# Down projection as seven block products, with its weight sums made in DRAM

## The chip, the cores and the metric

The kernel runs on one core of a Trainium2 chip. TensorE (PE) multiplies matrices, VectorE (DVE), ScalarE (ACT) and GpSimd (POOL) do elementwise work, and SyncE (SP) issues most transfers; POOL's queue issues others. 16 DMA engines carry all of them. PEld is TensorE's loading of stationary operands, which overlaps its matmuls. The time is the device time of one execution in microseconds (us), as the median of several runs. The profile is one further execution.

## The reference

One layer of an encoder block on 512 tokens of 1024 features in float32, with 16 learned meta tokens in front. Cut to what matters:

```
xn = rmsnorm(h); proj = xn @ w_in          # q, k, v of two kinds of attention, 8 heads each
y_sb = stick_breaking(...) @ w_br_sb       # sb heads
y_df = differential(...) @ w_br_df         # df heads
h = h + (gate0 * y_sb + gate1 * y_df) @ w_out
hn = rmsnorm(h)
h = h + (silu(hn @ w_ffn_gate) * (hn @ w_ffn_up)) @ w_ffn_down     # 1024 -> 2816 -> 1024
y = rmsnorm(h)                              # meta tokens dropped
```

The change is in the last product, the down projection: 512 tokens x 2816 by 2816 x 1024.

## The kernel before

The kernel works through the layer in stages: the eight sb heads, the eight df heads (the projections of the next head are cut into units that are popped between the steps of this one), the gates, the output projection, the FFN's gate and up products, the down projection, and the last norm.

Every float32 operand is split into a high and a low part of float32r, so that one product takes three matmuls (L227 high by high, L228 low activations by high weights, L229 high activations by low weights). For a weight tile ScalarE casts the high part (wh, L75) and VectorE subtracts it to get the low one (wl, L76). The same two lines split activations (da).

Weights come through one list, `stream`, in order of use. `stage_one` (L128 to L145) issues the next load on SP's queue into one of three buffers (wst). How far ahead loads and splits run is set by two constants, READY for split tiles and STAGE for loads. In the down projection `rows(("down", half, k0), ...)` makes 22 tiles of 128 x 2 x 512.

The down projection is the function `accumulate` (L1007), called once per half of the 1024 columns. Tokens are stationary, 128 at a time, and 512 columns of weights stream past: 22 k-tiles x 4 token tiles x 3 matmuls per half. The last token tile of the second half is cut into two pieces of 256 columns, so that the end of the kernel is short. VectorE adds the banks onto hres (L1036), ScalarE squares for the norm, POOL multiplies by the gain (L1260, L1261), ScalarE scales, SP writes the output.

The inputs of the down projection are the transposed activations aT, 22 k-tiles of 128 x 512 tokens, made by the FFN.

Also touched by what follows is `turn()` (L462 to L478), run once per head: TensorE transposes v, POOL copies 4 x 16 tail columns of vT into v_s (L475), TensorE transposes v_s (L476), and ScalarE copies the result:

```
for t in range(NQ):
    nc.gpsimd.tensor_copy(v_s[:, 32 * t:32 * t + NM], vT[:, (t + 1) * P:(t + 1) * P + NM])
nc.tensor.transpose(p5[:, 0:P], v_s, ident)
nc.scalar.copy(vf[:, 1], p5[:, 0:P])
```

Each engine works through its own instructions in order. Up to L921 the order of PE, DVE and ACT is written out by hand; after that a scheduler orders each engine, and it orders POOL and SP throughout. POOL's queue carries the y parts (L731 writes, L733 adds onto them in DRAM) and the loads of hres (L1004). A transfer on POOL's queue signals one of eight completion semaphores in turn (DMASW0 to DMASW7 in the order shown below).

Of the kernel before, what the change touches and what calls it, by code (L numbers as in the profile page):

```python
# [40 lines left out]
def block_kernel(ctx: ExitStack, tc: tile.TileContext, x, meta, norm_mix_g, w_in, w_gate, b_gate,  # L41
# [15 lines left out]
    def mm_tile():  # L57
        return ps_mm.tile([P, 512], F32, tag="mm", name="mm")
# [4 lines left out]
    def z_tile():  # L63
        return ps_z.tile([P, 2, 512], F32, tag="z", name="z")
# [18 lines left out]
    def rows(key, view, c0, k0):  # L83
        stream.append((key, view, c0, 512, k0, k0 + 2))
# [27 lines left out]
    for f in range(NFF):  # L112
        cols(("fg", f), w_fg, f * P)
        cols(("fu", f), w_fu, f * P)
    for half in range(2):
        for k0 in range(0, NFF, 2):
            rows(("down", half, k0), w_fd, half * 512, k0)

    at_of = {c[0]: n for n, c in enumerate(stream)}
    first_ffn = at_of["fg", 1]  # L120
    staged, loaded = [], {}
    fpools = {}
    ops = {}
# [4 lines left out]
    def stage_one():  # L128
        n = len(staged)
        if n == len(stream):  # L130
            return False
        key, view, c0, cw, k0, k1 = stream[n]

        if key[0] == "fu" and key[1]:
            if "w" not in fpools:
                return False
            st = fpools["w"].tile([P, KT, P], F32, tag="wsu", bufs=2, name="wsu")
        elif sevens(key) and key[2] == 1:
            st = fpools["a"].tile([P, KT, P], F32, tag="wsu", name="wsu")
        else:  # L140
            st = wpool.tile([P, k1 - k0, cw], F32, tag="wst", bufs=3, name="wst")
        staged.append(st)
        for a, b in ((0, 4), (4, 8)) if n < 2 else ((0, k1 - k0),):
            nc.sync.dma_start(st[:, a:b], view[:, k0 + a:k0 + b, c0:c0 + cw])
        return True  # L145

    def stage(upto):
        while len(staged) < upto and stage_one():
            pass

    def parts(n):
        k, _, _, cw, k0, k1 = stream[n]
        loaded[k] = tuple(wpool.tile([P, k1 - k0, cw], F32R, tag=t, name=t) for t in ("wh", "wl"))
        return loaded[k]

    def generic(n):
# [67 lines left out]
    def mm3(ps, pairs, start=True, stop=True, skip=False):  # L224
        n = len(pairs)
        for i, (ah, al, bh, bl) in enumerate(pairs):
            nc.tensor.matmul(ps, lhsT=ah, rhs=bh, start=(start and i == 0), stop=False, skip_group_check=skip)  # L227
            nc.tensor.matmul(ps, lhsT=ah, rhs=bl, start=False, stop=False, skip_group_check=skip)  # L228
            nc.tensor.matmul(ps, lhsT=al, rhs=bh, start=False, stop=(stop and i == n - 1), skip_group_check=skip)  # L229
# [695 lines left out]
    for br in range(2):  # L925
        name, head = (("y_sb", sb_head), ("y_df", df_head))[br]
        if br:
            nc.gpsimd.memset(a_s, 0.0)
            y_out.append(xtp.tile([P, KT, SEQ], F32, tag="y_sb", name="y_out"))
        for h in range(NH):  # L930
            if (br, h) == (0, 0):
                tB["t"] = opool.tile([P, 2, 2, 4, HL], F32R, tag="y_df", name="tB", bufs=1)
                sums = sum_units()
            if (br, h) == (0, 4):
                df_constants()
            if h % 2 == 0:
# [67 lines left out]
        nc.gpsimd.dma_start(hres[:, t], xv[:, t])  # L1004
    ssq = [small.tile([P, 2], F32, tag=f"ssq{t}", bufs=2, name="ssq") for t in range(NQ)]

    def accumulate(pool, name, act, nk, half, tail, done, banks, pieces=None):  # L1007
# [6 lines left out]
        extra = z_tile()[:, 0] if pieces else None  # L1014

        def step(k, t, c0, c1):
# [3 lines left out]
            mm3((acc[t] if c0 == 0 else extra)[:, c0:c1],  # L1020
                [(ah[:, q], al[:, q], wh[:, k % 2, c0:c1], wl[:, k % 2, c0:c1])], k == 0, k == nk - 1)


        def cuts(t):
            return ((0, 256), (256, 512)) if t == NQ - 1 and pieces else ((0, 512),)

        for k in range(nk - tail):
            for t in range(NQ):
                for c0, c1 in cuts(t):
                    step(k, t, c0, c1)  # L1030
        for t in range(NQ):
            for c0, c1 in cuts(t):
                for k in range(nk - tail, nk):
                    step(k, t, c0, c1)
                cs = slice(half * 512 + c0, half * 512 + c1)
                nc.vector.tensor_tensor(hres[:, t, cs], hres[:, t, cs], (acc[t] if c0 == 0 else extra)[:, c0:c1], op=ALU.add)  # L1036
                sq = pool.tile([P, 512], F32, tag="y_sb", bufs=2, name="sq")
                s0, s1 = ssq[t][:, 0:1], ssq[t][:, 1:2]
                nc.scalar.activation(sq[:, c0:c1], hres[:, t, cs], AF.Square, accum_out=(s1 if half else s0))
                if half == 0:  # L1040
                    nc.vector.tensor_scalar(s0, s0, 1.0 / D, EPS, op0=ALU.mult, op1=ALU.add)
                elif c1 < 512:
                    nc.vector.scalar_tensor_tensor(s0, s1, 1.0 / D, s0, op0=ALU.mult, op1=ALU.add)
                if pieces:
                    pieces(t, cs)
# [90 lines left out]
    with tc.tile_pool(name="ffn", bufs=1) as fp:  # L1136
# [10 lines left out]
        jobs += [(generic, n) for n in range(at_of["down", 0, 0], len(stream))]  # L1147
        made = {"n": 0}

        def ready(upto):  # L1150
# [56 lines left out]
        first(2)  # L1207
        first_out(2)
        dw, acts = None, []

        def act_parts(upto):

            for i in range(len(acts), min(2 * NFF, upto)):
                pool, tag, bufs = ((dw, "da", 4), (fw, ("wsu", "s21")[i % 2], 2))[i % 8 < 4]
                a = pool.tile([P, 2, SEQ], F32R, tag=tag, bufs=bufs, name="da")
                split(a[:, 0], a[:, 1], aT[:, i % NFF])
                acts.append(a)

        def act(half, k):
            act_parts(half * NFF + k + 3)  # L1220
            return acts[half * NFF + k][:, 0], acts[half * NFF + k][:, 1]

        for f in range(1, NFF):
            ready(at_job(c2, f) + 3)
# [19 lines left out]
        fpools["down"] = down_weights  # L1244
        ov = out[0].rearrange("(t p) d -> p t d", p=P)

        def finish(t):
# [7 lines left out]
        outs = []  # L1255

        def gained(t, cs):
            if len(outs) == t:
                outs.append(dw.tile([P, D], F32, tag="outs", name="outs", bufs=2))
                nc.gpsimd.tensor_tensor(outs[t][:, 0:512], hres[:, t, 0:512], gF[:, 0:512], op=ALU.mult)  # L1260
            nc.gpsimd.tensor_tensor(outs[t][:, cs], hres[:, t, cs], gF[:, cs], op=ALU.mult)  # L1261

        ssq = [small.tile([P, 2], F32, tag=f"ssq{t}", bufs=2, name="ssq") for t in range(NQ)]
        accumulate(dw, "down", act, NFF, 0, 0, lambda t: None, "z")
        accumulate(dw, "down", act, NFF, 1, 6, finish, "mm", gained)
        inner.close()


# [27 lines left out]
```

## Time and profile before

| what | value |
|---|---|
| median of 3 runs | 987.93 us (987.78 to 987.96) |
| span of the profiled execution | 987.0 us |
| PE busy | 963.9 us (98%) |
| DVE busy | 675.5 us (68%) |
| ACT busy | 572.6 us (58%) |
| POOL busy | 166.4 us (17%) |
| DMA, 16 engines, SP's queue q1 | 30.0% |
| DMA, POOL's queue q0 | 12.5% |
| first to last matmul of the down projection | 855.3 to 979.0 us |

"Busy" is the time in which an engine executed. The chain that ended last is followed back from the last instruction, each step to what released it. A row of a group gives line, engine, operation, output and input, their shapes, count, then busy time and mean of one, then idle time of the engine before these instructions and what ended it. A row of the timeline gives start, length, engine, line, operation, and in brackets the idle time before and its releaser.

### The profile page before, as it was taken

Reading aid. Unit: us, or ns where it says so; the run is one execution under the profiler, and the core shown is the slowest. Engines: PE = TensorE matmul, PEld = TensorE weight load, DVE = VectorE, ACT = ScalarE, POOL = GpSimd, SP = SyncE. Lnnn points to the kernel's source line nnn. Section 1 sums busy time; section 2 is a strip of 40 time slices with the busy share of each in tenths; the row PEclk is TensorE's granted clock in tenths of the full one; section 3 lists DMA queues with packets and bytes.
Section 4 is the critical chain, followed back from the end, with each engine's and each line's share of the span. In section 5 each row is a group of like instructions: output and inputs, shape, how many; then the busy total and the mean of one; then the engine's idle time right before and its main releaser. Section 6 shows DMA issues by size and latency. Waiting matters only on the chain.

```text
span 987.0 us, 16198 instructions
## 1 busy us (share of the span) xinstructions
PE 963.9 (98%) x6213; PEld 869.3 (88%) x6213; DVE 675.5 (68%) x1244; ACT 572.6 (58%) x1091; POOL 166.4 (17%) x216
## 2 busy tenths in 40 slices
PE   7999999999999999999999999989999999999996
PEld 4998888898899998899878888879999999988885
DVE  8898687766566876667724433798888888754644
ACT  5666666666566666666763433675555555743533
POOL 4010111111243322442224320000000000000103
PEclk9999999999999999999999999999999999999999
DMA  7312434455565533656659623232434333333212
GB/s 217 86 43 65 128 102 112 95 125 130 129 130 129 130 113 124 129 117 140 130 136 287 195 90 103 64 107 87 128 87 119 97 110 105 110 104 107 86 43 86
DMA packets 140240, 114.12 MB, mean 116 GB/s; under 512 B 4961, under 2 KB 115714, under 8 KB 140162
## 3 DMA queue, kind: packets, MB, share of 16 engines
q1 hardware_dynamic: 129810, 89.29, 30.0%
q0 software_dynamic: 10192, 23.73, 12.5%
q8 instruction: 49, 0.80, 0.3%
q14 instruction: 29, 0.24, 0.1%
q10 hardware_dynamic: 160, 0.07, 0.0%
HBM read 89.87 MB, written 18.87 MB: 110 GB/s over the span
## 4 chain that ended last, share of the span: by engine, by line
PE 88%; DVE 6%; ACT 4%; DMA 1%; issue 1%; POOL 0%; SPq 0%; DVEq 0%; ACTq 0%; POOLq 0%
PE mm L229 20%; PE mm L227 20%; PE mm L228 20%; PE z L227 6%; PE z L229 6%; PE z L228 6%; PE z L638 1%; PE z L637 1%; PE tr L493 1%; PE tr L469 1%; PE z L493 1%; ACT wh L75 1%; DVE s L576 1%; PE z L521 1%; DVE wl L76 0%
## 5 line engine op out<-in xcount | busy, mean ns | idle before, releaser
L76 DVE TENSOR_TENSOR wl<-wst,wh 128x1024 fp32r<-128x1024 f32 (+1 forms) x150 | 169.3, 1133 | 110.6 <-ACT wh L75 110.5
L75 ACT CAST wh<-wst 128x1024 fp32r<-128x1024 f32 (+1 forms) x150 | 146.0, 973 | 124.6 <-PE mm L228 68.4
L227 PE MATMUL mm<-xT_h,wh 128*128 128x264 f32 (+2 forms) x656 | 214.3, 327 | 0.2 <-ACT xT_h L831 0.2
L228 PE MATMUL mm<-xT_l,wh 128*128 128x264 f32 (+2 forms) x656 | 213.6, 326 | 0.4 <-DVE xT_l L832 0.3
L229 PE MATMUL mm<-xT_h,wl 128*128 128x264 f32 (+2 forms) x656 | 212.8, 324 | 0.0
L227 PEld LDWEIGHTS mm<-xT_h,wh 128*128 128x128 f32 x656 | 123.9, 189 | 10.0 <-ACT xT_h L831 1.0
L228 PEld LDWEIGHTS mm<-xT_l,wh 128*128 128x128 f32 x656 | 123.7, 189 | 10.0 <-DVE xT_l L832 0.6
L229 PEld LDWEIGHTS mm<-xT_h,wl 128*128 128x128 f32 x656 | 123.7, 189 | 9.9
L228 PE MATMUL mm<-hT_l,wh 128*128 128x256 f32 x284 | 80.5, 284 | 0.7 <-DVE hT_l L1079 0.7
L227 PE MATMUL mm<-hT_h,wh 128*128 128x256 f32 x284 | 80.1, 284 | 0.6 <-DVE sg L1174 0.6
L229 PE MATMUL mm<-hT_h,wl 128*128 128x256 f32 x284 | 80.1, 283 | 0.0
L641 DVE CUSTOM_DVE_ANT_0 pr<-z,bias 128x144 f32<-128x144 f32 (+3 forms) x64 | 30.9, 502 | 34.9 <-PE z L638 34.8
L228 PEld LDWEIGHTS mm<-hT_l,wh 128*128 128x128 f32 x284 | 53.7, 189 | 1.2 <-DVE hT_l L1079 1.1
L227 PEld LDWEIGHTS mm<-hT_h,wh 128*128 128x128 f32 x284 | 53.4, 189 | 0.9 <-DVE sg L1174 0.8
L475 POOL COPY v_s<-vT 128x16 f32<-128x16 f32 x64 | 26.3, 440 | 162.5 <-DVE vT L405 78.2
L229 PEld LDWEIGHTS mm<-hT_h,wl 128*128 128x128 f32 x284 | 53.6, 189 | 0.0
L227 PE MATMUL mm<-o_h,wh 128*128 128x512 f32 x128 | 53.1, 415 | 0.0
L229 PE MATMUL mm<-o_h,wl 128*128 128x512 f32 x128 | 50.8, 397 | 0.0
L228 PE MATMUL mm<-o_l,wh 128*128 128x512 f32 x128 | 50.1, 392 | 0.3 <-DVE o_l L709 0.3
L1260 POOL TENSOR_TENSOR outs<-hres,gF 128x512 f32<-128x512 f32 x4 | 5.1, 1291 | 262.2 <-DVE hres L1036 261.3
L227 PE MATMUL mm<-t_h,wh 128*128 128x256 f32 x168 | 47.5, 282 | 1.3 <-ACT wh L75 1.0
L228 PE MATMUL mm<-t_l,wh 128*128 128x256 f32 x168 | 47.2, 281 | 1.1 <-DVE t_l L1094 1.1
(328 smaller groups left out, 2538.5 us busy)
## 6 DMA issues: line engine op xcount, KB each, us to landing
wst<-in_w_in_dram SPq DMA_DIRECT2D x40, 512.0 KB, 4.7
wst<-in_w_ffn_gate_dram SPq DMA_DIRECT2D x22, 512.0 KB, 3.8
wst<-in_w_ffn_down_dram SPq DMA_DIRECT2D x22, 512.0 KB, 3.5
wsu<-in_w_ffn_up_dram SPq DMA_DIRECT2D x21, 512.0 KB, 3.8
y_df<-y_out POOLq DMA_DIRECT2D x32, 256.0 KB, 5.1
wst<-in_w_gate_dram SPq DMA_DIRECT2D x16, 512.0 KB, 5.4
wst<-in_w_br_sb_dram SPq DMA_DIRECT2D x8, 512.0 KB, 4.7
wst<-in_w_br_df_dram SPq DMA_DIRECT2D x8, 512.0 KB, 3.8
```

What stands on the lines that cost most here:

```text
L75: (hi_copy or nc.scalar.copy)(hi, src)
L76: (lo_eng or nc.vector).tensor_tensor(lo, src, hi.bitcast(F32), op=ALU.subtract)
L227: nc.tensor.matmul(ps, lhsT=ah, rhs=bh, start=(start and i == 0), stop=False, skip_group_check=skip)
L228: nc.tensor.matmul(ps, lhsT=ah, rhs=bl, start=False, stop=False, skip_group_check=skip)
L229: nc.tensor.matmul(ps, lhsT=al, rhs=bh, start=False, stop=(stop and i == n - 1), skip_group_check=skip)
L469: nc.tensor.transpose(pt[:, j * P:(j + 1) * P], vT[:, j * P:(j + 1) * P], ident)
L475: nc.gpsimd.tensor_copy(v_s[:, 32 * t:32 * t + NM], vT[:, (t + 1) * P:(t + 1) * P + NM])
L493: nc.tensor.transpose(pt[:, (t - j) * P:(t - j + 1) * P], blocks(t, j * P, (j + 1) * P), ident)
L521: nc.tensor.matmul(ps.rearrange("p (t q) -> p t q", q=P)[:, :, lo_rows:P], lhsT=vf[:, 1], rhs=a_s[:, 0:4 * qn], start=False, stop=True)
L576: nc.vector.tensor_tensor_scan(f, f, f, 0.0, op0=ALU.add, op1=ALU.bypass)
L637: nc.tensor.matmul(o, lhsT=q[c][:, qs], rhs=k[c][:, 0, k0:k1], start=True, stop=False)
L641: nc.vector.tensor_tensor_reduce(po, zz, bb, scale=1.0, scalar=-3.0e38, op0=ALU.add, op1=ALU.max, accum_out=mx[:, t, c:c + 1])
```

## The change

The down projection becomes a 2 x 2 x 2 block product made of seven products instead of eight. Blocks are 11 k-tiles x 512 columns of weights (a) and 256 tokens x 11 k-tiles of activations (b):

```
DOWN = (("a11", "b11", 0), ("a12", "b21", 1), ("s1", "t1", 2), ("s2", "t2", 0), ("s4", "b22", 2), ("s3", "t3", 0),
        ("a22", "t4", 0))
```

Each entry is weights, activations, and the accumulator that takes the product. Four weight blocks are sums: s1 = a21 + a22, s3 = a21 + a11, s2 = a11 + s1, s4 = a12 + s2. They are made in DRAM by transfers on POOL's queue: 24 copies out of w_ffn_down into the DRAM tiles (d...) and 24 that accumulate (8 block jobs of 6 tiles each; five tiles are of 512 KB, the sixth of 256 KB). The code pops one such job after each unit of the heads (`background`). Four activation blocks are sums t1 to t4, made by VectorE in place over aT and in a buffer t2f (24 operations, `token_sum`).

The weight tiles of the down projection are now 42 (35 of 128 x 1024, 7 of 128 x 512) instead of 22, loaded from w_ffn_down or from the sums, and staged in the three wst buffers and four more (`slots`, in the space of xT_l). The activations are split per pair of k-tiles and 256 tokens (`act_parts`), 42 splits instead of 44, with ScalarE's copy scaled and VectorE's subtraction a scalar_tensor_tensor. hres is updated from the accumulators as products end (`to_res`, 16 operations instead of 9), and norms and outputs follow per token tile.

The diff, cut to its core:

```
+    def sum_job(to, of, k0, add):
+        src = raw_down(of, k0) if of in raw_at else w_sum[of, k0][:, 0:min(2, NK - k0)]
+        dst = w_sum[to, k0][:, 0:min(2, NK - k0)]
+        if add:
+            nc.gpsimd.dma_start(dst, src, accum_op=ALU.add, max_dma_last_dim=2048)
+        else:
+            nc.gpsimd.dma_start(dst, src)
+
+    background = [(to, of, k0, i > 3) for i, (to, of) in enumerate(
+        (("s1", "a21"), ("s2", "a11"), ("s3", "a21"), ("s4", "a12"), ("s1", "a22"), ("s3", "a11"), ("s2", "s1"), ("s4", "s2")))
+        for k0 in DK]
...
             for n in head(h, d, o[0][:, h % 2], o[1][:, h % 2]):
                 for _ in range(min(n, len(units))):
                     units.pop(0)()
+                    if background:
+                        sum_job(*background.pop(0))
...
+                a = pool.tile([P, 2, 2, 256], F32R, tag=tag, bufs=bufs, name="da")
+                src, sign = block(b, k0), -1.0 if b == "t2" else 1.0
+                nc.scalar.activation(a[:, 0, 0:n], src, AF.Copy, scale=sign)
+                nc.vector.scalar_tensor_tensor(a[:, 1, 0:n], src, sign, a[:, 0, 0:n].bitcast(F32), op0=ALU.mult, op1=ALU.subtract)
...
+        def token_sum(name, k0):
+            b11, b12, b21, b22 = block("t1", k0), block("t3", k0), block("b21", k0), block("b22", k0)
+            to, x, y, op = {"t1": (b11, b11, b12, ALU.subtract), "t2": (block("t2", k0), b11, b22, ALU.add),
+                            "t3": (b12, b22, b12, ALU.subtract), "t4": (b21, block("t2", k0), b21, ALU.subtract)}[name]
+            nc.vector.tensor_tensor(to, x, y, op=op)
...
-            stage(at_of[key] + STAGE)
+            stage(at_of[key] + READY + 6)
...
+        def to_res(t, cs, ps, op):
+            nc.vector.tensor_tensor(hres[:, t, cs], hres[:, t, cs], ps, op=op)
...
+        zt = [z_tile() for _ in range(2)]
+        acc = [[zt[0][:, 0], zt[0][:, 1]], [mm_tile(), mm_tile()], [zt[1][:, 0], zt[1][:, 1]]]
+        extra = mm_tile()
...
+        def step(i, j, t, c0=0, c1=512, start=False, stop=False):
+            w, b, e, k0 = order_of[i]
+            act_parts(i + 3)
+            wh, wl = weights(("down", w, k0))
+            a, q = acts[i], slice(t * P, (t + 1) * P)
+            ps = extra if c0 else acc[e][t]
+            mm3(ps[:, c0:c1], [(a[:, 0, j, q], a[:, 1, j, q], wh[:, j, c0:c1], wl[:, j, c0:c1])], start, stop, True)
...
+        for ph, (w, b, e) in enumerate(DOWN):
+            i0 = ph * len(DK)
+            steps = [(i0 + k // 2, k % 2) for k in range(NK)]
+            tail = 6 if ph == 6 else 3
...
+            for k in range(0, NK - tail, 2):
+                i = i0 + k // 2
+                while todo and len(todo) > 24 - i / 1.55:
+                    token_sum(*todo.pop(0))
+                for t in range(2):
+                    for j in range(min(2, NK - tail - k)):
...
```

How the built order of POOL changes. Before, at the copies of heads 1 to 3 (head 0's stand ahead; numbers behind names are buffers, [waits ...] are semaphores):

```order
L475 COPY v_s_138<-vT_560 128x16 [waits Pool_49] x2
L475 COPY v_s_138<-vT_864 128x16 [waits DVE_49]
L475 COPY v_s_138<-vT_864 128x16 [waits DVE_49,Pool_49]
L475 COPY v_s_138<-vT_864 128x16 [waits Pool_49] x2
L475 COPY v_s_138<-vT_1131 128x16 [waits DVE_49]
L475 COPY v_s_138<-vT_1131 128x16 [waits DVE_49,Pool_49]
L475 COPY v_s_138<-vT_1131 128x16 [waits Pool_49] x2
L731 DMA y_sb_0_80<-sg_1373 128x512 [waits Activation_49]
```

With the change, at head 2's copies (vT_896; the line of v_s is now L509, L138 is an adding transfer):

```order
L509 COPY v_s_164<-vT_896 128x16 [waits DVE_49]
L138 DMA ds2_4_84<-ds1_4_78 256x512 [waits DMASW6_49]
L138 DMA ds2_6_85<-ds1_6_79 256x512 [waits DMASW7_49]
L138 DMA ds2_8_86<-ds1_8_80 256x512 [waits DMASW0_49]
L138 DMA ds2_10_87<-ds1_10_81 128x512 [waits DMASW1_49]
L138 DMA ds4_0_94<-ds2_0_82 256x512 [waits DMASW4_49,DMASW2_49]
L138 DMA ds4_2_95<-ds2_2_83 256x512 [waits DMASW5_49,DMASW3_49]
L138 DMA ds4_4_96<-ds2_4_84 256x512 [waits DMASW6_49]
L138 DMA ds4_6_97<-ds2_6_85 256x512 [waits DMASW7_49]
L138 DMA ds4_8_98<-ds2_8_86 256x512 [waits DMASW0_49]
L509 COPY v_s_164<-vT_896 128x16 [waits DVE_49,Pool_49]
L509 COPY v_s_164<-vT_896 128x16 [waits Pool_49] x2
```

All 48 transfers stand in POOL's order between the start and head 3's copies: 18 of them ahead of head 0's last copies, 33 ahead of head 1's, 47 ahead of head 2's and 48 ahead of head 3's.

VectorE's order in the down projection. Before (wl: low part of weights, da: low part of activations):

```order
L76 TENSOR_TENSOR wl_9724<-wst_9552,wh_9723 128x1024 [waits DMAHW1_49,Activation_49]
L76 TENSOR_TENSOR da_9775<-aT_6990,da_9775 128x512 [waits PE_49,Activation_49]
L76 TENSOR_TENSOR da_9790<-aT_6990,da_9790 128x512 [waits Activation_49]
L76 TENSOR_TENSOR wl_9760<-wst_9685,wh_9759 128x1024 [waits DMAHW2_49,Activation_49]
L76 TENSOR_TENSOR da_9811<-aT_6990,da_9811 128x512 [waits PE_49,Activation_49]
```

With the change, in the first products (L1254 splits activations, L1261 makes token sums):

```order
L1261 TENSOR_TENSOR t2f_9712<-aT_7064 128x512
L76 TENSOR_TENSOR wl_9818<-slots_9711,wh_9817 128x1024 [waits DMAHW5_49,Activation_49]
L1254 SCALAR_TENSOR_TENSOR da_9893<-aT_7064,da_9893 128x512 [waits PE_49,Activation_49]
L1261 TENSOR_TENSOR t2f_9712<-aT_7064 128x512
L76 TENSOR_TENSOR wl_9833<-wst_9734,wh_9832 128x1024 [waits DMAHW0_49,Activation_49]
L1254 SCALAR_TENSOR_TENSOR da_9914<-aT_7064,da_9914 128x256 [waits PE_49,Activation_49]
L1261 TENSOR_TENSOR t2f_9712<-aT_7064 128x512 x3
```

A weight tile used to serve four token tiles and now serves two, so wl stands twice as often per matmul, and token sums stand between the splits.

More of the change, by code (lines that the diff above doesn't have):

```diff
@@ L132, in stage_one @@
         key, view, c0, cw, k0, k1 = stream[n]
+        if n >= first_down + 3 and "slots" not in fpools:
+            return False
         if key[0] == "fu" and key[1]:
@@ L140, in stage_one @@
         else:
-            st = wpool.tile([P, k1 - k0, cw], F32, tag="wst", bufs=3, name="wst")
+            slot = (n - first_down) % 7 - 3 if n >= first_down else -1
+            if slot < 0:
+                st = wpool.tile([P, 1024 // cw, cw], F32, tag="wst", bufs=3, name="wst")[:, 0:k1 - k0]
+            else:
+                st = fpools["slots"][:, slot, 0:k1 - k0]
         staged.append(st)
@@ L152, in parts @@
         k, _, _, cw, k0, k1 = stream[n]
-        loaded[k] = tuple(wpool.tile([P, k1 - k0, cw], F32R, tag=t, name=t) for t in ("wh", "wl"))
+        loaded[k] = tuple(wpool.tile([P, 1024 // cw, cw], F32R, tag=t, name=t)[:, 0:k1 - k0] for t in ("wh", "wl"))
         return loaded[k]
@@ L1005, in block_kernel, with accumulate @@
     ssq = [small.tile([P, 2], F32, tag=f"ssq{t}", bufs=2, name="ssq") for t in range(NQ)]
-    def accumulate(pool, name, act, nk, half, tail, done, banks, pieces=None):
+    def accumulate(pool, name, act, nk, half, tail, done, banks):
         if banks == "z":
@@ L1013, in accumulate, with step @@
             acc = [mm_tile() for _ in range(NQ)]
-        extra = z_tile()[:, 0] if pieces else None
-        def step(k, t, c0, c1):
+        def step(k, t):
             ah, al = act(half, k)
@@ L1019, in step @@
             q = slice(t * P, (t + 1) * P)
[L1020 to L1025, printed above, removed]
+            mm3(acc[t], [(ah[:, q], al[:, q], wh[:, k % 2], wl[:, k % 2])], k == 0, k == nk - 1)
+        cs = slice(half * 512, (half + 1) * 512)
         for k in range(nk - tail):
             for t in range(NQ):
-                for c0, c1 in cuts(t):
-                    step(k, t, c0, c1)
+                step(k, t)
         for t in range(NQ):
[L1032 to L1045, printed above, removed]
+            for k in range(nk - tail, nk):
+                step(k, t)
+            nc.vector.tensor_tensor(hres[:, t, cs], hres[:, t, cs], acc[t], op=ALU.add)
+            sq = pool.tile([P, 512], F32, tag="y_sb", bufs=2, name="sq")
+            s0, s1 = ssq[t][:, 0:1], ssq[t][:, 1:2]
+            nc.scalar.activation(sq, hres[:, t, cs], AF.Square, accum_out=(s1 if half else s0))
+            if half == 0:
+                nc.vector.tensor_scalar(s0, s0, 1.0 / D, EPS, op0=ALU.mult, op1=ALU.add)
             done(t)
@@ L1146, in block_kernel @@
             jobs += [(c2, f), (c3, f)] + [(c1, f + 1)] * (f + 1 < NFF) + [(c4, f)]
-        jobs += [(generic, n) for n in range(at_of["down", 0, 0], len(stream))]
+        jobs += [(generic, n) for n in range(first_down, len(stream))]
         made = {"n": 0}
@@ L1240, in down_weights @@
             ready(jobs.index((generic, at_of[key])) + READY)
-            stage(at_of[key] + STAGE)
+            stage(at_of[key] + READY + 6)
             return loaded[key]
         fpools["down"] = down_weights
+        fpools["slots"] = xtp.tile([P, NM + KT * SEQ], F32, tag="xT_l", name="slots")[:, NM:].rearrange(
+            "p (a b c) -> p a b c", a=4, b=2)
+        part["t2"] = xtp.tile([P, NM + KT * SEQ], F32, tag="xT_h", name="t2f")[:, NM:NM + NK * 256].rearrange(
+            "p (k t) -> p k t", t=256)
         ov = out[0].rearrange("(t p) d -> p t d", p=P)
@@ L1253, in finish, with summed @@
             nc.sync.dma_start(ov[:, t, 512:D], o[:, 512:D])
-        outs = []
+        outs = {}
+        ssq = [small.tile([P, 2], F32, tag=f"ssq{t}", bufs=2, name="ssq") for t in range(NQ)]
+        D1, D2 = slice(0, 512), slice(512, D)
+        def to_res(t, cs, ps, op):
+            nc.vector.tensor_tensor(hres[:, t, cs], hres[:, t, cs], ps, op=op)
+        def summed(t, cs):
+            sq = dw.tile([P, 512], F32, tag="y_sb", bufs=2, name="sq")[:, 0:cs.stop - cs.start]
+            s0, s1 = ssq[t][:, 0:1], ssq[t][:, 1:2]
+            nc.scalar.activation(sq, hres[:, t, cs], AF.Square, accum_out=(s1 if cs.start else s0))
+            if cs.start == 0:
+                nc.vector.tensor_scalar(s0, s0, 1.0 / D, EPS, op0=ALU.mult, op1=ALU.add)
+            elif cs.stop < D:
+                nc.vector.scalar_tensor_tensor(s0, s1, 1.0 / D, s0, op0=ALU.mult, op1=ALU.add)
@@ L1257, in gained @@
         def gained(t, cs):
-            if len(outs) == t:
-                outs.append(dw.tile([P, D], F32, tag="outs", name="outs", bufs=2))
-                nc.gpsimd.tensor_tensor(outs[t][:, 0:512], hres[:, t, 0:512], gF[:, 0:512], op=ALU.mult)
+            if t not in outs:
+                outs[t] = dw.tile([P, D], F32, tag="outs", name="outs", bufs=2)
+                nc.gpsimd.tensor_tensor(outs[t][:, D1], hres[:, t, D1], gF[:, D1], op=ALU.mult)
             nc.gpsimd.tensor_tensor(outs[t][:, cs], hres[:, t, cs], gF[:, cs], op=ALU.mult)
-        ssq = [small.tile([P, 2], F32, tag=f"ssq{t}", bufs=2, name="ssq") for t in range(NQ)]
@@ L1264, in block_kernel @@
-        accumulate(dw, "down", act, NFF, 0, 0, lambda t: None, "z")
-        accumulate(dw, "down", act, NFF, 1, 6, finish, "mm", gained)
+        zt = [z_tile() for _ in range(2)]
+        acc = [[zt[0][:, 0], zt[0][:, 1]], [mm_tile(), mm_tile()], [zt[1][:, 0], zt[1][:, 1]]]
+        extra = mm_tile()
+        add, sub = ALU.add, ALU.subtract
+        todo = [(n, k0) for n in ("t1", "t2", "t3", "t4") for k0 in DK]
+        def step(i, j, t, c0=0, c1=512, start=False, stop=False):
[5 more added lines that the diff above has]
+            mm3(ps[:, c0:c1], [(a[:, 0, j, q], a[:, 1, j, q], wh[:, j, c0:c1], wl[:, j, c0:c1])], start, stop, True)
@@ new lines, in block_kernel @@
+        fresh = {0: 0, 1: 1, 2: 2}
+        for ph, (w, b, e) in enumerate(DOWN):
+            i0 = ph * len(DK)
+            steps = [(i0 + k // 2, k % 2) for k in range(NK)]
+            tail = 6 if ph == 6 else 3
+            first_k = (lambda k: k == 0) if fresh[e] == ph else (lambda k: False)
+            for k in range(0, NK - tail, 2):
[4 more added lines that the diff above has]
+                    for j in range(min(2, NK - tail - k)):
+                        if ph == 6 and t:
+                            step(i, j, t, 0, 256)
+                            step(i, j, t, 256, 512, start=k + j == 0)
+                        else:
+                            step(i, j, t, start=first_k(k + j))
+            for t in range(2):
+                for c0, c1 in ((0, 256), (256, 512)) if ph == 6 and t else ((0, 512),):
+                    for k, (i, j) in enumerate(steps[NK - tail:]):
+                        if t == 0 and j == 0:
+                            while todo and len(todo) > 24 - i / 1.55:
+                                token_sum(*todo.pop(0))
+                        step(i, j, t, c0, c1, stop=k == tail - 1)
+                    ps = extra if c0 else acc[e][t]
+                    cs = slice(512 + c0, 512 + c1)
+                    if w == "a12":
+                        to_res(t, D1, acc[0][t], add)
+                        to_res(t, D1, ps, add)
+                        summed(t, D1)
+                    elif w == "s1":
+                        to_res(2 + t, D2, ps, sub)
+                    elif w == "s2":
+                        to_res(2 + t, D1, ps, add)
+                    elif w == "s4":
+                        to_res(2 + t, D1, ps, add)
+                        summed(2 + t, D1)
+                    elif w == "s3":
+                        with tc.high_priority(offset=EVAC):
+                            to_res(2 + t, D2, ps, sub)
+                            if t:
+                                to_res(t, slice(768, D), ps[:, 256:512], sub)
+                        summed(2 + t, D2)
+                        gained(2 + t, D2)
+                        finish(2 + t)
+                    elif w == "a22":
+                        to_res(t, cs, ps[:, c0:c1], sub)
+                        summed(t, cs)
+                        gained(t, cs)
+                        if c1 == 512:
+                            finish(t)
```

37 lines of the change are left out of this document (28 added, 9 removed).

## The prediction

> **What bounds the kernel now.** I read the busy times first, then the chain that ended last.
>
> ```profile
> PE 963.9 (98%) x6213; PEld 869.3 (88%) x6213; DVE 675.5 (68%) x1244; ACT 572.6 (58%) x1091; POOL 166.4 (17%) x216
> PE 88%; DVE 6%; ACT 4%; DMA 1%; issue 1%; POOL 0%; SPq 0%; DVEq 0%; ACTq 0%; POOLq 0%
> ```
>
> TensorE is busy for 963.9 of 987.0 us and is 88% of the chain. So a matmul less is worth its time, where nothing else takes its place, and every us in which TensorE is held anywhere is lost for good. The change touches two places: the down projection at the end, and the first hundred us, where POOL's queue now gets 48 transfers. The windows of the start show what runs there (window, length, busy PE, PEld, DVE, ACT, POOL with counts, granted clock, share of the 16 DMA engines, GB/s):
>
> ```profile
> 0.00:20.00 20.00, 15.06 (x73) 9.63 (x74) 15.53 (x44) 11.72 (x29) 10.37 (x19) 0.91 0.83 243
> 20.00:40.00 20.00, 17.78 (x132) 17.26 (x131) 17.12 (x42) 11.49 (x25) 2.23 (x3) 0.91 0.27 77
> 40.00:60.00 20.00, 19.68 (x139) 17.99 (x138) 19.11 (x28) 12.37 (x24) 1.04 (x4) 1.00 0.19 54
> 60.00:80.00 20.00, 19.17 (x135) 17.22 (x134) 18.64 (x30) 14.68 (x27) 2.23 (x5) 1.00 0.22 63
> 80.00:85.40 5.40, 5.40 (x42) 4.92 (x40) 5.35 (x11) 4.13 (x6) 0.00 (x0) 1.00 0.16 61
> ```
>
> TensorE is nearly full, POOL nearly empty, and the DMA engines are some 20% busy: there seems to be room for the transfers. The timeline at 85 us shows what POOL does there all the same:
>
> ```profile
> 85.44 1.33 POOL L475 COPY v_s<-vT 128x16 f32<-128x16 f32 x3 [12.34 <-DVE vT L405]
> 86.83 0.33 PE L476 MATMUL tr<-ident,v_s 128*128 128x128 f32 x1 [1.02 <-POOL v_s L475]
> ```
>
> Once per head POOL copies the tail of v into v_s, and TensorE transposes v_s in its own fixed order. Even now TensorE waits 1.02 us for it. A late v_s stops TensorE.
>
> **The down projection.** The steps of 512 columns are read between two L227 rows with 12 matmuls from the one to the other, those of 256 columns from a full window of the FFN (columns as above):
>
> ```profile
> 863.04 0.39 PE L227 MATMUL z<-wh,da 128*128 128x512 f32 x1
> 865.76 0.39 PE L227 MATMUL z<-wh,da 128*128 128x512 f32 x1
> 700.00:760.00 60.00, 60.00 (x505) 60.00 (x504) 50.36 (x79) 32.94 (x55) 0.00 (x0) 1.00 0.37 106
> ```
>
> That is 2.72/12 = 0.2267 us, and 60/505 = 0.119 us. Before, 22 k-tiles x 4 token tiles x 2 halves x 3 = 528 matmuls, of which 66 are cut into two: 462 x 0.2267 + 132 x 0.119 = 104.7 + 15.7 = 120.4 us. After, 7 products x 11 k-tiles x 2 token tiles x 3 = 462, of which 33 are cut: 429 x 0.2267 + 66 x 0.119 = 97.3 + 7.9 = 105.2 us. TensorE saves **15.2 us**.
>
> VectorE pays for it. Its groups in the stage, by form (busy, mean ns | idle before):
>
> ```profile
> L76 DVE TENSOR_TENSOR wl<-wst,wh 128x1024 fp32r<-128x1024 f32 x18 | 22.6, 1257 | 39.5 <-ACT wh L75 39.5
> L76 DVE TENSOR_TENSOR da<-aT,da 128x512 fp32r<-128x512 f32 x39 | 26.6, 688 | 7.9 <-ACT da L75 7.9
> L1036 DVE TENSOR_TENSOR hres<-hres,mm 128x512 f32<-128x512 f32 x3 | 2.1, 686 | 7.6 <-PE mm L229 7.6
> L1036 DVE TENSOR_TENSOR hres<-hres,mm 128x256 f32<-128x256 f32 x1 | 0.4, 414 | 0.0
> ```
>
> Before: 22 x 1.257 + 44 x 0.688 + 8 x 0.686 = 63.4 us, idle for ScalarE in between. After: 35 weight tiles x 1.257 + 7 halves x 0.69 = 48.8; 35 activation tiles x 0.688 + 7 x 0.42 = 27.0; 20 token sums x 0.686 + 4 x 0.41 = 15.4; 13 updates of hres x 0.686 + 3 x 0.41 = 10.1; some 6 us of small work at the end (my estimate). Together **107 us against TensorE's 105**. About 10 us of that lie ahead of the first matmul or behind the last, so VectorE has some 97 us in a stage of 105. But it works in order and waits for ScalarE's halves and for transfers (7.9 us behind 39 activation tiles alone). It can't give back what it waits, and the pool of weights is as deep as before. Bounds of the gain: 15 us if every wait is hidden, 0 if VectorE's 107 and its waits, some 13 us, set the stage. I take the middle, **7.5 us**.
>
> **The weight sums.** Forty-eight transfers enter POOL's order, each of 512 KB (the last of every six half that): 24 copies from DRAM to DRAM, then 24 that add onto them. The built order (shown with the change) puts 47 of them ahead of three of head 2's v_s copies, and gives each the completion semaphore of the transfer eight before it. POOL waits at such a transfer until the older one has landed; what stands behind waits too. That this is how POOL behaves, the trace of before shows where hres is loaded behind the y parts, which have the same form (DRAM, accumulating):
>
> ```profile
> 526.96 0.88 POOL L733 DMA_DIRECT2D y_df<-y_out  x1 [0.45 <-issue]
> 532.71 0.59 POOL L1004 DMA_DIRECT2D hres<-in_x_dram  x1 [4.87 <-DMA y_df<-y_out]
> ```
>
> POOL stood 4.87 us for a transfer to land. The 47th here (an s4 tile, added from an s2 tile) waits for the 41st, whose result it reads. So head 2's v_s can't be made before 41 transfers have moved. Of the first 41, 24 are copies (4 of them halves, so 22 full) and 17 add (2 halves: 16 full).
>
> What one costs, no row shows: nothing in the trace copies DRAM to DRAM. The nearest are loads of 2 KB rows (860 to 960 us), and the y parts' accumulations out of SBUF (515 to 518, 518 to 533 and 167 to 179 us): packets, MB, share of the 16 engines.
>
> ```profile
> q1 hardware_dynamic: 4624, 8.91, 26.3%
> q0 software_dynamic: 206, 0.38, 100.8%
> q0 software_dynamic: 791, 1.43, 58.0%
> q0 software_dynamic: 567, 1.04, 61.1%
> ```
>
> Loads: 26.3% x 100 us / 8.91 MB = 2.95 us per MB, or 1.55 us per 512 KB (0.524 MB). Accumulations: 100.8% x 3 / 0.38 = 8.0; 58.0% x 15 / 1.43 = 6.1; 61.1% x 12 / 1.04 = 7.1 us per MB; together 19.1 us for 2.85 MB, 6.7 per MB, or **3.5 us** per 512 KB, the lowest 3.2. A copy lies between a load (1.55) and an accumulation (3.5), since it writes DRAM but doesn't read what it writes; I take **2.3**, nearer to the load. An adding transfer takes 3.2 at the least and, if its source costs a load on top, 3.5 + 1.55 = 5.05 at the most. I take 3.5, the row with the same write side.
>
> The Trainium skill, in "DMA: Bandwidth & Descriptors", section "Latency and other measured facts", gives copies within HBM about 207 to 214 GB/s at their full rate. That would be an estimate of 2.45 us per 512 KB, and 22 x 0.15 = 3 us more than my sum; no run here shows it yet.
>
> The loads of the same time want the same engines. By the windows above, 0.83 x 20 + 0.27 x 20 + 0.19 x 20 + 0.22 x 20 + 0.16 x 5.4 = 31 us of all 16. Then the start of head 2's v_s is 2 us (POOL's first issues) + 31 + 22 x 2.3 + 16 x 3.5 + 3 (landing and the last issue) = 2 + 31 + 50.6 + 56 + 3 = **142.6 us instead of 85.4: 57.2 us late**. The first loads of x and weights are late by the sums ahead of them too, and heads 0 and 1 have 18 and 33 sums ahead of their last copies, but those are parts of the same 57 us: the transfers don't wait for TensorE. Nothing gives it back, since TensorE is 98% busy afterwards. Later, one sum stands ahead of head 3's copies, and then none. Of the 133 transfers that POOL now issues the other 85 are as before.
>
> Also added: 20 more SP loads in the down projection, 42 tiles (20.2 MB) instead of 22 (11.5 MB). At 26.3% x 20.2/11.5 = 46% of the engines I cost them at nothing; they are hidden under its matmuls. If a transfer there took twice its time, they would just set the stage's end.
>
> Sum against the profiled execution: 987.0 + 57.2 - 7.5 = 1036.7 us of span. The median of the runs shown is 0.9 us above that span, so about **1038 us**.
>
> **The rivals.**
>
> *The sums are hidden, and the kernel is faster.* If the 41 transfers land in what the engines have free, 85.4 - 31 - 5 = 49 us, v_s isn't late. For it, DMA is 20% busy from 20 us on. Against it, 22 copies even at a load's 1.55 us take 34 us, and the 15 left give an adding transfer 0.94 us, under a third of the lowest row. Time: 988 - 15 to 988 - 7.5, about 973 to 981. The same page's section "Anatomy of one DMA — SWDGE (gpsimd) path" leads here: 2.0 us fixed, which overlaps between transfers, and 436 GB/s would make 1.2 us of each, 46 us in all. The accumulations' rows, at 3.2 us and more, speak against it for more than half of them. Chance 0.10.
>
> *Hidden, and no gain either.* VectorE's 107 us and its waits fill the stage as in the lower bound above: about 988. Chance 0.04.
>
> *The sums are dearer.* With 3.5 us a copy and 5.05 us an adding transfer: 2 + 31 + 77 + 80.8 + 3 = 194, 108 us late, about 1089. For it, every adding transfer here reads DRAM twice. Against it, reading and writing go on side by side in the rows of loads and stores at once. Chance 0.13 for more than 1068.
>
> *POOL's order is not what counts.* If the wait of the 47th didn't hold the copies, DMA traffic alone would slow the first loads; that is the first rival's time again and has no chance of its own.
>
> **How the numbers follow.** Forecast 0.73, the rivals 0.10, 0.04 and 0.13. The low end takes 1.55 and 3.2 us: 2 + 31 + 34.1 + 51.2 + 3 = 121.3, 35.9 us late, with the full gain of 15: 988 + 35.9 - 15 = 1009; 5 us less if the loads partly run beneath the sums' latencies: 1004. The high end takes 5.05 us for an adding transfer at my price of a copy: 24.8 us more, 1063, and 5 us for a gain that is only 2.5: 1068. A measurement of this kernel tells about 0.2% (2 us) from no change. Faster 0.10, within it 0.04, slower 0.86.
>
> **What would show it.** Head 2's v_s copies near 143 us, with POOL waiting for the DMA of an s4 tile before them; TensorE idle for tens of us at the transposes of v_s between 40 and 145 us, and its granted clock below 1.00 for longer than the 40 us of now; q0 with some 23 MB more; 0.2267 us a step in the down projection, VectorE full there and the stage some 7 us shorter. It is wrong if POOL never waits for DMA before 90 us, if TensorE's idle time there is named for loads of weights instead, or if an adding transfer takes under 1 us.

## The result, and the profile after

The changed kernel takes **1014.35 us** (median of 5 runs) against 987.93 before: ratio 1.0259, 95% interval 1.0246 to 1.0272, so 26 us slower. Forecast were 1038 us, in a range of 1004 to 1068. One of the five, the one that was profiled, ran at a granted clock of 0.745 and took 1191.56 us; the ratio is of the other four, and the profile below is of the same kernel run again (median 1016.1 us, ratio 1.0272, interval 1.0253 to 1.0292).

Its busy times and its chain by engine:

```profile
PE 960.2 (94%) x6114; PEld 863.9 (85%) x6114; DVE 705.2 (69%) x1293; ACT 584.5 (58%) x1109; POOL 205.1 (20%) x264
PE 80%; DMA 7%; DVE 6%; ACT 5%; issue 1%; SPq 0%; DVEq 0%; ACTq 0%
```

TensorE's share of the chain fell from 88% to 80%, and DMA's rose from 1% to 7%: 7% of 1016 us is some 70 us in which the chain waits for transfers. The windows of the start show where (columns as before):

```profile
20.00:40.00 20.00, 17.28 (x134) 16.18 (x134) 18.29 (x43) 12.99 (x30) 13.37 (x18) 1.00 1.02 346
40.00:60.00 20.00, 15.22 (x95) 13.56 (x94) 7.28 (x12) 4.89 (x10) 9.30 (x14) 0.92 1.01 305
60.00:80.00 20.00, 15.18 (x87) 13.95 (x87) 18.57 (x29) 11.18 (x23) 5.99 (x8) 0.74 0.85 156
80.00:100.00 20.00, 17.03 (x116) 15.21 (x114) 4.91 (x9) 9.76 (x16) 5.36 (x8) 1.00 1.09 199
100.00:120.00 20.00, 10.75 (x57) 9.70 (x58) 18.45 (x29) 8.40 (x18) 11.40 (x15) 0.66 1.11 217
120.00:140.00 20.00, 8.80 (x53) 8.21 (x52) 4.47 (x8) 4.98 (x8) 0.27 (x1) 0.66 0.75 151
140.00:160.00 20.00, 20.00 (x127) 17.67 (x126) 15.53 (x25) 12.17 (x24) 2.55 (x6) 1.00 0.34 106
```

The DMA engines are full or nearly so up to about 130 us, where they were 20% to 40% busy before. (A share above 1.00 means that the packets' times overlap, so shares are not exact engine time.) From 100 to 140 us TensorE has 57 and 53 instructions where it had 122 and 137, at a granted clock of 0.66. From 140 us on it is full again. So the place of the loss is the one forecast. Its cause isn't. The longest pieces of the chain in the first 150 us (start, length, what):

```profile
38.77 18.09 DMA wst<-in_w_in_dram
82.34 17.85 DMA wsu<-in_w_in_dram
116.19 16.12 DMA wsu<-in_w_in_dram
```

Three loads of the heads' weights, 16 to 18 us each, are what TensorE waited for. Such loads took 4.4 and 5.3 us (512 KB, first 110 us) in the kernel before:

```profile
wst<-in_w_in_dram SPq DMA_DIRECT2D x10, 512.0 KB, 4.4
wsu<-in_w_in_dram SPq DMA_DIRECT2D x3, 512.0 KB, 5.3
```

The three are (18.1 - 4.4) + (17.9 - 5.3) + (16.1 - 5.3) = 37 us longer. What makes up the rest of the loss wasn't taken apart. And the copies that the prediction was about, in the timeline after, with the VectorE operation that made the last of head 2's v:

```profile
114.56 0.43 DVE L439 TENSOR_TENSOR vT<-mm,qq 128x264 f32<-128x264 f32 x1 [0.18 <-PE mm L263]
115.72 0.89 POOL L138 DMA_DIRECT2D ds<-ds  x1 [2.98 <-DMA ds<-ds]
116.28 0.78 POOL L509 COPY v_s<-vT 128x16 f32<-128x16 f32 x3
117.12 0.33 PE L510 MATMUL tr<-ident,v_s 128*128 128x128 f32 x1 [1.38 <-POOL v_s L509]
```

Head 2's v_s stands behind the 47th sum, as foretold, and is 31 us late, not the 57 forecast. But TensorE waits only 1.38 us for it (1.02 before). It was late itself by then: v, which is copied into v_s, was made no sooner than 115.0 us (85.3 before), so the sum ahead in POOL's order cost the copies about 1 us.

### The profile page after: what moved, and what is told of

Read it like the earlier page. It is cut to its first block, busy times and chain, and to the rows that moved or that the text cites. A ratio compares the mean times of both kernels' runs of the same rounds, so it can differ in the third digit from the quotient of the medians.

```text
span 1189.8 us, 16178 instructions
## 1 busy us (share of the span) xinstructions
PE 1155.2 (97%) x6114; PEld 977.4 (82%) x6114; DVE 714.9 (60%) x1293; ACT 592.5 (50%) x1109; POOL 203.3 (17%) x264
## 4 chain that ended last, share of the span: by engine, by line
PE 89%; DMA 5%; DVE 4%; ACT 2%; issue 0%; SPq 0%; DVEq 0%; ACTq 0%
PE mm L263 20%; PE mm L262 20%; PE mm L261 20%; PE z L261 7%; PE z L262 7%; PE z L263 7%; DMA wsu<-in_w_in_dram 3%; DMA wst<-in_w_in_dram 2%; PE z L671 1%; PE z L672 1%; PE tr L527 1%; PE z L527 1%; PE tr L503 1%; PE z L555 1%; DVE s L610 1%; ACT wh L75 0%
## 5 line engine op out<-in xcount | busy, mean ns | idle before, releaser
L261 PE MATMUL mm<-xT_h,wh 128*128 128x264 f32 (+2 forms) x656 | 248.1, 378 | 0.2 <-PE mm L822 0.2
L263 PE MATMUL mm<-xT_h,wl 128*128 128x264 f32 (+2 forms) x656 | 244.8, 373 | 0.0
L262 PE MATMUL mm<-xT_l,wh 128*128 128x264 f32 (+2 forms) x656 | 243.1, 371 | 0.5 <-DVE xT_l L866 0.5
L262 PEld LDWEIGHTS mm<-xT_l,wh 128*128 128x128 f32 x656 | 137.4, 209 | 19.8 <-DVE xT_l L866 0.8
L263 PEld LDWEIGHTS mm<-xT_h,wl 128*128 128x128 f32 x656 | 135.8, 207 | 21.3
L261 PEld LDWEIGHTS mm<-xT_h,wh 128*128 128x128 f32 x656 | 135.3, 206 | 20.2 <-ACT xT_h L865 1.0
L261 PEld LDWEIGHTS mm<-hT_h,wh 128*128 128x128 f32 x284 | 63.0, 222 | 0.8 <-DVE sg L1198 0.8
L263 PEld LDWEIGHTS mm<-hT_h,wl 128*128 128x128 f32 x284 | 63.3, 223 | 0.0
L261 PE MATMUL z<-wh,da 128*128 128x512 f32 (+1 forms) x132 | 58.4, 442 | 0.4 <-DVE hres L1304 0.4
L262 PE MATMUL z<-wl,da 128*128 128x512 f32 (+1 forms) x132 | 58.7, 445 | 0.0
L263 PE MATMUL z<-wh,da 128*128 128x512 f32 (+1 forms) x132 | 58.3, 446 | 0.0
## 6 DMA issues: line engine op xcount, KB each, us to landing
ds<-ds POOLq DMA_DIRECT2D x10, 512.0 KB, 16.7
```

## The experiments

Theory A is the one on record: POOL's order holds the v_s copies, and these hold TensorE. Theory B: the sums take the DMA engines, and the heads' weights come late. The kernel before was run beside each group; differences below are between medians of one group where not said otherwise.

**The change again** (no edit).

> The changed kernel once more, for a profile at full clock. The theory on record (POOL's order holds head 2's v_s copies, and so TensorE): about 1014 us, TensorE idle for some 25 to 35 us between 60 and 130 us, most of it named for POOL's v_s. The rival (the sums take the DMA engines, and the loads of the heads' weights come late): the same 1014 us, but the idle time ends at weight tiles whose loads took 10 us and more, and v_s ends under 6 us of it.

Measured: 1016.09 us. The idle time ends at weight loads of 16 to 18 us, and v_s ends 1.4 us of it: B's picture. But a chain names only what came last, so both were tested by taking them away.

**v_s on ScalarE.**

```
-                nc.gpsimd.tensor_copy(v_s[:, 32 * t:32 * t + NM], vT[:, (t + 1) * P:(t + 1) * P + NM])
+                nc.scalar.copy(v_s[:, 32 * t:32 * t + NM], vT[:, (t + 1) * P:(t + 1) * P + NM])
```

> The change with all copies into v_s on ScalarE, so that nothing of TensorE's path stands behind the sums in POOL's order; the sums themselves stay where they are. If POOL's order makes the loss: 980 to 990 us, all of the loss gone. If late weight loads make it: 1005 to 1014 us.

Measured: 1015.77 us, 0.3 us from the change itself. No copy into v_s stands behind the sums any more, and all of the loss is there. (Some of POOL's splits of the first weights, L875, still do; they and the issuing of two sums are under 5 us of the chain.) The chain of this kernel has the same three loads:

```profile
38.83 20.16 DMA wst<-in_w_in_dram
85.71 17.69 DMA wsu<-in_w_in_dram
113.99 17.25 DMA wsu<-in_w_in_dram
```

Head 2's v_s came no sooner there, at 117.36 us: ScalarE works in order too and had just stood 3.78 us for a load.

```profile
115.41 1.04 ACT L75 CAST wh<-wst 128x1024 fp32r<-128x1024 f32 x1 [3.78 <-DMA wst<-in_w_in_dram]
```

A falls as the cause of what was measured.

**No sums.**

```
+    raw_at |= {"s1": (0, 512), "s2": (0, 0), "s3": (0, 512), "s4": (NK, 0)}
-    background = [(to, of, k0, i > 3) for ...]
+    background = []
```

> The seven products without the 48 transfers; where a sum belongs, the kernel loads a raw block of weights of the same size, so the outputs are not the reference's. It times the down projection by itself. By the prediction 988 - 7.5 = 980 us, at most 988 (VectorE sets the stage), at least 973 (all of TensorE's 15 us). Both theories of the loss expect the same here.

Measured: 974.0 us against 988.97, ratio 0.9846 (0.9831 to 0.9861). The down projection gains 15.0 us, twice the 7.5 forecast, and the sums cost 1016.1 - 974.0 = 42.1 us in the changed kernel. The stage's first and last matmuls with da (tile view), its one window, and its two largest VectorE groups:

```profile
L259 PE MATMUL z<-wh,da x132: 277/389/499, 856.7 to 965.2; 128*128 128x512 f32 x121, 128*128 128x256 f32 x11
L261 PE MATMUL mm<-wh,da x33: 279/389/390, 875.3 to 966.6; 128*128 128x512 f32 x22, 128*128 128x256 f32 x11
850.00:970.00 120.00, 116.53 (x577) 97.93 (x576) 99.84 (x153) 73.40 (x119) 12.66 (x9) 1.00 0.53 173
L76 DVE TENSOR_TENSOR wl<-slots,wh 128x1024 fp32r<-128x1024 f32 x20 | 26.3, 1324 | 4.4 <-ACT wh L75 4.4
L1252 DVE SCALAR_TENSOR_TENSOR da<-aT,da 128x512 fp32r<-128x512 f32 x26 | 17.0, 683 | 0.0
```

From 856.7 to 966.6 is 109.9 us, where it took 123.7: 13.8 of the 15.0 us lie between the first matmul and the last, and about 1 us behind the last (6.9 us to the end of the span instead of 8.0). VectorE is busy for 99.84 of these 120 us, and for 91.6 of the stage's own 110, where 97 had been costed; but the waits feared are small: 4.4 us at the largest group, none at the activations, which waited 7.9 us for ScalarE before.

**The sums alone**, in the kernel before:

```
                     units.pop(0)()
+                    if background:
+                        sum_job(*background.pop(0))
```

> The kernel before with the 48 transfers added in the same loop of the heads, and their results read by nobody. The loss of the sums by itself: by the sum of the prediction 57 us (1045 us); by the measured total and a gain of 7.5 us in the down projection 34 us (1022 us). If the loss is not in the heads but in the down projection, 988 us.

Measured: 1027.56 us, 38.6 more than before. The first matmul of the down projection comes at 890.8 us instead of 855.3, and that stage takes the same 123.7 us as before. So the loss lies ahead of it, whatever the down projection does.

**Why a load takes 16 us.** In the change, packets, MB and share of the engines from 30 to 48 us (only copies), 85 to 125 us (only adding transfers) and 50 to 60 us, q0 the sums, q1 the loads:

```profile
q0 software_dynamic: 1323, 4.75, 74.8%
...
q0 software_dynamic: 3497, 6.71, 92.3%
q1 hardware_dynamic: 2804, 1.80, 18.6%
...
q0 software_dynamic: 812, 2.55, 86.1%
q1 hardware_dynamic: 781, 0.40, 17.0%
```

From 50 to 60 us the two queues moved 812 and 781 packets, one for one, but 2.55 and 0.40 MB: a load's packet is 512 B, a sum's 2 KB or more. From 85 to 125 us a packet of a sum took 0.923 x 40 x 16 / 3497 = 0.169 us, one of a load 0.186 x 40 x 16 / 2804 = 0.042. If an engine takes the queues in turn, a load of 1024 packets, 64 an engine, takes 64 x 0.211 = 13.5 us and some latency: the 16 to 18 us of the chain. The Trainium skill, in "DMA: Bandwidth & Descriptors", section "Queues, rings and completion order", states that a DMA engine goes round the queues that have work, packet by packet. Our 812 to 781 agree, if its packets, typically of 9 to 17 descriptors, are those that the trace counts; no run here shows that. While the two later loads of the chain run, the counts are near to each other too (1052 to 989 from 86 to 98 us, 517 to 522 from 124 to 130). They aren't where one queue has less to move: from 45 to 50 us it was 283 to 773, with the sums at 61% of the engines.

That can be tested by the size of a load's packets.

**Long rows with sums, and without.**

```
-            nc.sync.dma_start(st[:, a:b], view[:, k0 + a:k0 + b, c0:c0 + cw])
+            if view is w_in:
+                r = (b - a) // 4
+                c = min(c0, w_in.shape[2] - 512)
+                nc.sync.dma_start(st[:, a:b].rearrange("p k c -> p (k c)").rearrange("p (r c) -> p r c", c=512),
+                                  view[:, a // 4:a // 4 + r, c:c + 512])
+            else: ...                                   # as before
```

> The change with the same sums at the same place, but the heads' weight tiles are loaded in rows of 2 KB instead of 512 B (256 packets for 512 KB instead of 1024, from another place of w_in, so the outputs are not the reference's). If the DMA engines take packets of the two queues in turn, a load waits for one packet of a sum (0.17 us) at each of its own; with 16 packets an engine instead of 64 it lands after 4 to 8 us instead of 16 to 18, and the loss against the same kernel without sums falls from 42 us to under 15: 975 to 990 us. If what counts is that the engines are full for 130 us, whatever the rows, the loss stays: 1005 to 1016 us.

> The control for the long rows: the same loads in rows of 2 KB and no sums (raw blocks of weights in their places; outputs not the reference's). Both theories: 970 to 975 us, as without sums before (974.0), since those loads were 1% of the chain.

Measured: 997.96 us with sums, 973.67 without. The loss falls from 42.1 to 24.3 us though the engines are as full as before (shares of 1.02 to 1.12 from 40 to 120 us), so the size of a load's packets counts. It doesn't fall below 15. The profile says why: a long piece of its chain, and its wait of TensorE.

```profile
86.35 16.58 DMA ds<-ds
PE tr L516 <- POOL v_s L515: 10.1, 1, 10.1
```

With the loads sooner, theory A's wait comes up: the chain runs through a sum, POOL and v_s.

**Long rows, and v_s on ScalarE** (both edits together).

> The sums at their place in the change, loads of the heads in rows of 2 KB (outputs not the reference's) and the copies into v_s on ScalarE: both suspected causes taken away at once. Theory: with short waits for loads, POOL's order was what held the kernel with long rows and sums (998 us; TensorE waited 10.1 us for v_s there), so this one loses under 12 us against 973.7: 974 to 986 us. If POOL's order never mattered, as the run with v_s on ScalarE alone (1016) could be read: 995 to 1000 us.

Measured in the next group: 989.88 us (ratio to before 1.0012), against 973.67 (0.9843) without sums: by the ratios 1.69% or 16.7 us. That is 8 us less than with long rows alone, so POOL's order does hold TensorE once loads don't. The time lies between the two ranges expected. What is left in the chain are loads again:

```profile
36.28 11.06 DMA wst<-in_w_in_dram
92.57 8.10 DMA wsu<-in_w_in_dram
```

In the two by two of these runs the sums cost 42.1 us (as changed), 41.8 (v_s moved), 24.3 (long rows), 16.7 (both). v_s alone is worth nothing, behind long rows 8 us: two limits side by side, of which only the one that ends later is seen. Sixteen packets an engine should take 16 x (0.17 + 0.09) = 4 us and some latency, where 8 to 11 were seen; what makes up the rest wasn't tried and stays open.

**All sums at the start of the FFN.** `sum_job` leaves the heads' loop, and:

```
-        nc.gpsimd.dma_start(gF, norm_final_g.rearrange(...))
+        ins = nc.gpsimd.dma_start(gF, norm_final_g.rearrange(...))
+        with tc.issue_after(ins.ins):
+            for job in background:
+                sum_job(*job)
```

> All 48 sums together, but at the start of the FFN, behind the last transfer of POOL there; POOL has nothing else to do until the end, so no copy can be held by its order. The FFN's weights come in 512 B rows too, two tiles per 13 us. If alternating packets make the loss: two tiles take 2 x 64 x 0.21 = 27 us instead of 13 while the sums last, some 100 us, so 25 to 50 us are lost: 1000 to 1025 us. If the loss belongs to the start of the kernel (empty buffers, a cold clock): 974 to 980 us.

Measured: 1042.26 us, 68 more than without sums, and more than any theory gave. POOL had nothing else to do there, so A has no part. Its chain, and the loads from 655 to 780 us:

```profile
657.90 18.68 DMA wsu<-in_w_ffn_up_dram
680.11 20.99 DMA wsu<-in_w_ffn_up_dram
706.10 19.41 DMA wsu<-in_w_ffn_up_dram
...
wsu<-in_w_ffn_up_dram SPq DMA_DIRECT2D x6, 512.0 KB, 18.8
wst<-in_w_ffn_gate_dram SPq DMA_DIRECT2D x6, 512.0 KB, 27.7
```

An FFN tile lands after 19 and 28 us instead of 3.8. One step of the FFN takes 24 us (706.1 to 730.5 in the chain), near the 27 us that were given for two tiles; a step is 10 us otherwise, not the 13 that I had put down. Some 5 steps at 14 us more are the 68.

**Three a head.** `sum_job` leaves the loop; in `turn`, behind the copies into v_s:

```
+            turns.append(key)
+            if len(turns) > 1:
+                with tc.issue_after(ins.ins):
+                    for _ in range(min(len(background), 6 if len(turns) == 2 * NH else 3)):
+                        sum_job(*background.pop(0))
```

> The same 48 sums in groups of three, each behind one head's copies into v_s, from the second head on (the last group has six). By the theory of alternating packets, a load next to three sums is 5 to 8 us later, which the three weight buffers cover, and the whole gain of the down projection stays: 974 to 979 us. If the sums cost engine time that TensorE must wait for, their 97 us spread over the heads still cost 20 us or more: 990 to 1010 us.

Measured: 981.97 us, ratio 0.9929 (0.9908 to 0.9949). The same 48 transfers with the same bytes cost 8 us instead of 42, and the kernel is now 0.7% faster than before. It is above the 974 to 979 expected. Two loads of the first heads still stand in its chain:

```profile
65.59 8.03 DMA wsu<-in_w_in_dram
172.01 11.68 DMA wsu<-in_w_in_dram
```

**Spread wider**, with nothing in the first five heads:

```
-            if len(turns) > 1:
+            if len(turns) > 5:
                 with tc.issue_after(ins.ins):
-                    for _ in range(min(len(background), 6 if len(turns) == 2 * NH else 3)):
+                    for _ in range(2):
...
+            if f > 1:                                   # in the FFN's loop
+                pin = small.tile([P, 1], F32, tag="pin", name="pin")
+                ins = nc.gpsimd.tensor_copy(pin, aT[:, f, 0:1])
+                with tc.issue_after(ins.ins):
+                    for _ in range(min(len(background), 1 + (f % 2))):
+                        sum_job(*background.pop(0))
```

> The same 48 sums spread wider than three a head: two behind each head's copies into v_s from the sixth turn on (22), then one or two behind each step of the FFN (26), pinned there by a copy of one column of aT on POOL. With three a head the first 200 us lost some 6 us; here nothing runs there. If the loss is a matter of how many packets stand beside a load: 974 to 978 us. If each sum costs by itself: 980 to 985 us, as with three a head.

Measured: 979.47 us, ratio 0.9893 (0.9878 to 0.9908): between the two ranges expected. In the profiles the first matmul of the down projection comes 1.7 us later than without sums (858.4 against 856.7 us). The larger part of what was left is in that stage, which takes 112.4 us instead of 109.9: its matmuls were slower, in the same order.

**The same with a pin of 64 bytes, and three a head again.**

```
-                pin = small.tile([P, 1], F32, tag="pin", name="pin")
-                ins = nc.gpsimd.tensor_copy(pin, aT[:, f, 0:1])
+                pin = small.tile([P, 16], F32, tag="pin", name="pin")
+                ins = nc.gpsimd.tensor_copy(pin[:, 0:1], aT[:, f, 0:1])
```

> The sums spread as in the run before, with one difference: the small tile into which POOL copies is 64 bytes per partition instead of 4. In that run a 512-column step of the down projection took 0.231 us, not 0.227, with the same matmuls in the same order. If the 16 bytes by which four such tiles shift all later tiles in SBUF make the matmuls slower, the step is 0.227 again and the time 975 to 977 us; if the cause is another (an activation or a transfer of that stage), 979 to 980 us as before.

> The kernel with three sums a head again, beside the one with the spread sums on the same chip, so that the two can be compared: 980 to 983 us, and 0.227 us a step in the down projection.

Measured: **975.77 us**, ratio 0.9868 (0.9853 to 0.9882), and 980.63 for three a head (0.9912, 0.9896 to 0.9929). The first is the best version: 13 us faster than the kernel before, 2 us above the kernel without sums. A step of three a head was 0.227 us, as expected. By the ratios the larger pin is worth 2.5 us, and the intervals of the two spread kernels just overlap (0.9878 and 0.9882), so the step is better evidence than the time. Matmuls with da in the tile view, min/median/max in ns, with the pin of 4 bytes and then of 64:

```profile
L262 PE MATMUL z<-wh,da x132: 279/393/504, 858.4 to 969.4; 128*128 128x512 f32 x121, 128*128 128x256 f32 x11
```

```profile
L262 PE MATMUL z<-wh,da x132: 277/389/501, 857.2 to 966.4; 128*128 128x512 f32 x121, 128*128 128x256 f32 x11
```

These 132 stretch over 111.0 us with the small pin and 109.2 with the larger. The median is 389 ns in every other kernel here, also in those measured on the same chip as the small pin, so the chip isn't the reason.

## Why the prediction was right, and where it was wrong

- **Slower, by the sums, in the first 140 us: right.** The time lies in the range, at its lower end. The rival that the sums are hidden falls with the run of the sums alone (38.6 us).
- **The price of a copy, 2.3 us: too high.** 0.748 x 18 us / 4.75 MB = 2.83 us per MB, so 1.49 us for 512 KB: just below the lower end that a load gave (1.55). By these shares a copy that writes DRAM cost no more than a load. The Trainium skill's 207 to 214 GB/s ("DMA: Bandwidth & Descriptors", section "Latency and other measured facts"), by which the estimate was 2.45 us, were further off: 4.75 MB in 0.748 x 18 us are 352 GB/s.
- **The price of an adding transfer, 3.5 us: too high.** 0.923 x 40 / 6.71 = 5.50 us per MB, or 2.88 us, below the lowest row (3.2). The shares of both queues add up to 111% in that window, so this is good to some 10%. The Trainium skill's fit of bytes over 436 GB/s ("DMA: Bandwidth & Descriptors", section "Anatomy of one DMA — SWDGE (gpsimd) path"), an estimate of 1.2 us, isn't reached by either. The prediction said of it that the rows of adding transfers speak against it for more than half of the transfers; they are 16 of 38 full ones.
- **The sum for head 2's v_s: right in form.** With these prices it is 2 + 31 + 22 x 1.49 + 16 x 2.88 + 3 = 115 us, and the copies ran at 116.28 us. POOL waited at the 47th sum, as said. But v itself came at 115.0, so the agreement doesn't show that the sums set the time.
- **"A late v_s stops TensorE" as the cause: wrong.** This is the step that failed. The prediction put the loads into the sum as 31 us of engine time and dropped them as a cause of their own; the fourth rival even gave them no chance. They came 11 to 14 us late each, since their 512 B packets alternate with the sums' packets, and TensorE lost its time there before it came to v_s. Moving v_s to ScalarE gave 0.3 us. That the time fell into the range is in part luck: with the measured prices the same sum makes v_s 115 - 85.4 = 30 us late, and with the measured gain 988 + 30 - 15 = 1003 us, below the range. Prices that were too high stood in for the loads that were left out. The prediction had named this sign itself: idle time that ends at loads of weights.
- **"Nothing gives it back": right.** From 140 us on TensorE is full, and the loss stays: 42 us at the end (1016.1 against 974.0).
- **The gain of the down projection, 7.5 us: half of what came.** Of TensorE's 15.2 us 13.8 arrived, and about 1 us more came behind the last matmul, which the prediction didn't have. VectorE's time was costed well (91.6 us in the stage for 97), but its waits for ScalarE, which the middle value assumed, were small. The change stages weights in seven buffers instead of three; whether that is why wasn't tested.
- **The total.** Forecast +57.2 - 7.5 = +50; measured +42.1 - 15.0 = +27. Two errors with one sign: sums that were priced too high and a gain that was halved.

## What to carry to other kernels

Transfers in the background are not free because the DMA engines look 20% busy: count packets, not bytes. Here a load in rows of 512 B that shared the engines with packets of 2 KB and more waited for about one of theirs at each of its own. So issue such work a few at a time, pinned behind instructions that are spread over the program. And when two limits end near each other, take away each alone and both together before believing the chain or one's own sum: here the one alone gave 0.3 us, and 8 us once the other was smaller.

## What the runs showed of the hardware that was not expected

- By the queues' shares, a copy from DRAM to DRAM took 1.49 us of all 16 engines for 512 KB, no more than a load into SBUF (1.55); an adding transfer took 2.88.
- 48 transfers (23 MB) cost 42 us together at the start, 68 us together in the FFN, 8 us at three a head, and 2 us spread over heads and FFN.
- With a tile of 4 instead of 64 bytes a partition, not used by any matmul, the matmuls of the down projection were 1% to 2% slower (a median of 393 against 389 ns, 111.0 against 109.2 us for the same 132) and the kernel some 2.5 us slower by the ratios. Each has one trace. Four such tiles shift what is placed behind them by 16 bytes. That the alignment of the operands does it is argued, not shown.
